# Hybrid attention and mLSTM block: attention one unit further ahead, mLSTM from unit 6, first output weights through four raw tiles

## The chip, the cores and the metric

One core of a Trainium2 chip runs the whole layer as one launch. The metric is the device time of one execution in microseconds (us), taken as the median of several runs. The engines are named as in the profile: PE is TensorE (matmuls), PEld its weight loads, DVE is VectorE, ACT is ScalarE, POOL is GpSimd, SP is the engine whose queue issues nearly all transfers.

## What is computed

The input is 2048 tokens of 1024 values. After an RMS norm one projection feeds two mixers; their outputs, each times a gate, are concatenated and projected back onto the residual, and a last RMS norm follows.

```python
h = rmsnorm(x, norm_g)
u = einsum("bsd,de->bse", h, w_in)
q_a, k_a, v_a, z_a, x_m, o_m, z_m = split(u, cuts)
# (A) 8 heads: causal windows of dilation 1, 4 and 16 with ALiBi, mixed by their softmax denominators
for window, dilation in ((128, 1), (512, 4), (2048, 16)):
    o, l = dilated_window_attention(q_a, k_a, v_a, window, dilation, slopes)
wts = softmax(stack(lses), axis=0)
att = sum(wts * stack(outs)) * silu(z_a)
# (B) 4 heads of an mLSTM matrix memory, chunk by chunk
hm = mlstm_chunkwise(q_m, k_m, v_m, log_i, log_f)
mls = groupnorm(sigmoid(o_m) * hm) * silu(z_m)
y = x + einsum("bse,ed->bsd", concatenate([att, mls]), w_out)
out = rmsnorm(y, final_g)
```

## The kernel before

**Stages.** First the input projection runs as a long stream of float32 products on PE, and its results go to DRAM. Then come three kinds of work that share the engines: attention, mLSTM, and the half of the output projection that belongs to the mLSTM. Last comes the other half of the output projection with the final norm.

**Attention** (`attention`) runs over 256 units, 32 for each of 8 heads; a unit is one block of 128 queries against a near window or a far one. For a unit `qk` makes the scores: three matmuls into the PSUM tile `pq` (two buffers), a DVE instruction that adds the bias and takes the row's extreme (L752), and an exponential on ACT (L754), which leaves the weights in the score tile `s` (three buffers). `flip` transposes them on PE (L762) into the PSUM tile `pt` (two buffers, which mLSTM uses too), and ACT or DVE copies them to `p` (L767, L765). `pv` multiplies them with the values (L780). In pass i of the loop stand `qk` of unit i, `flip` of unit i-2 and `pv` of unit i-3. After a head, `head_stats` and `head_merge` mix its two windows; `spread` broadcasts a row of weights over the partitions with a matmul whose stationary operand is the tile `sel` (L828).

**mLSTM** (`mlstm`) runs over 16 chunks of 128 tokens, two units a chunk, and `norm` closes each chunk with a chain of small DVE instructions. It is a generator of 400 steps.

**The early half of the output projection** (`early`) multiplies the mLSTM's output with the lower half of `w_out`, first for the left 512 columns (n=0), then for the right ones (n=1). It loads 8 weight tiles of 128x512 for each n into raw tiles `wor` (two buffers), and `split` makes of each a high part on ACT (L98) and a low part on DVE (L99) in `we`. The 16 blocks of mLSTM output come in halves the same way, through `wor` into `me` (three buffers). A block is 8 steps of three matmuls (L1142 to L1144) into `pu`; x is added and the sum goes to `y_d`. Between n=0 and n=1 the weights are changed.

**What sets the order.** The main loop at the end weaves the generators. `start` (18) attention units go alone; then, up to unit `end` (180), each attention unit is followed by its share of the 400 mLSTM steps; `lag` (3) units go alone; then 2.6 steps of `early` follow each attention unit, 2.0 after the last one. A step that yields 0 ends the share of its unit. From pass 230 on, `load_wo` also loads the upper half of `w_out`, through `wor` as well (and later a third raw tile, `qh`). This order is only a priority: a planner orders the instructions of each engine by it and by the times at which it expects operands and buffers to be ready, so an instruction that is ready may pass others that stand ahead of it in the text. On the chip each engine then runs its instructions strictly in the planned order. The pool `woB` of `early` takes over the memory of the mLSTM's pool `mp`, and `mp` that of the projection's pool (`ph`).

Of the kernel before, what the change touches and what calls it, by code (L numbers as in the profile page):

```python
# [8 lines left out]
F32 = mybir.dt.float32  # L9
# [18 lines left out]
def kernel(  # L28
# [693 lines left out]
    def qk(at, d, u):  # L722
        R, b = u
        g, r = b // 4, b % 4
        kh, kl, bl, st = d["kh"], d["k"], d["bl"], d["st"]
        ps = pq.tile([128, 512], F32, name="pq")
        if R:
            n = (g + 1) * 128
            bias = bl[:, 768 - n:768]
            col = 32 + b  # L730
            ks = lambda t: t[:, r * 512:r * 512 + n]
        else:
            n = 256 if b else 128
            bias = bl[:, 256 - n:256]
            col = b
            ks = lambda t: t.rearrange("p (r b j) -> p b r j", r=4, b=16)[:, max(b - 1, 0):b + 1]

        def keys(t):
            k = ks(t)
            if n == 128:  # L740
                k = k[:, None] if R else k
                k = k.to_broadcast([k.shape[0], 2, *k.shape[2:]])
            return k

        qhr, qlr = (d["qr", g][:, i, g % 2] for i in range(2))
        qh, ql = (t[:, r * 128:(r + 1) * 128] for t in ((qhr, qlr) if R else (qhi[:, g % 2], qt[:, g])))
        w = max(n, 256)
        nc.tensor.matmul(ps[:, 0:w], qh, keys(kh), start=True, stop=False)  # L748
        nc.tensor.matmul(ps[:, 0:w], qh, keys(kl), start=False, stop=False)  # L749
        nc.tensor.matmul(ps[:, 0:w], ql, keys(kh), start=False, stop=True)  # L750
        s = at.tile([128, 512], F32, name="s", bufs=3)
        nc.vector.tensor_tensor_reduce(s[:, :n], ps[:, :n], bias, 1.0, 3e38, ALU.add, ALU.min,  # L752
                                       accum_out=st[:, col:col + 1])
        nc.scalar.activation(s[:, :n], s[:, :n], AF.Exp, bias=st[:, col:col + 1], scale=-1.0,  # L754
                             accum_out=st[:, 16 + col:17 + col])
        return s, n
# [31 lines left out]
    def head_stats(at, d):  # L788
        h = d["h"]
        ps = pt.tile([128, 512], F32, name="pt")  # L790
        nc.tensor.transpose(ps[:64, :128], d["st"], ident)
        sr = at.tile([128, 512], F32, name="s", bufs=3)[:64, :128]
        nc.vector.tensor_copy(sr[:32].rearrange("p (r j) -> p r j", r=4), ps[:32, :128].rearrange("p (j r) -> p r j", r=4))
        nc.vector.tensor_copy(sr[32:], ps[32:64, :128])
        sd = st_d[h]
# [29 lines left out]

    def spread(d, n, q):
        pw = pt.tile([128, 512], F32, name="pt")
        nc.tensor.matmul(pw, sel[:, 2 * q + n // 2], d["wr"][:, n % 2 * 512:n % 2 * 512 + 512], start=True, stop=True)  # L828
        return residues(pw)

    def head_merge(at, d):
# [20 lines left out]
    def attention(at):  # L852
# [6 lines left out]
        D_ = {}  # L859
        S_ = {}  # L860
        P_ = {}
        for i in range(len(units) + 3):
            if i < len(units):
                h, u = units[i]
                if i == 0:
# [3 lines left out]
                    D_[0]["kh"] = kh  # L869
                    qk_split(D_[0], 0)  # L870
                S_[i] = qk(at, D_[h], u)
            if 0 <= i - 2 < len(units):
                h, u = units[i - 2]
                s, n = S_[i - 2]
                P_[i - 2] = flip(at, D_[h], u, s, n)
            if i >= 3:
                h, u = units[i - 3]
                pv(D_[h], u, P_.pop(i - 3), S_.pop(i - 3)[1])
            if i < len(units):
                h, (R, b) = units[i]  # L880
                if R and b % 4 == qlag and h + 1 < AH:
# [9 lines left out]
                if R and b % 4 == slag:  # L891
                    if b < 12:
                        qk_split(D_[h], b // 4 + 1)
                    elif h + 1 < AH:
                        qk_split(D_[h + 1], 0)
            if i % 32 == 3 and i > 31:
                stats = head_stats(at, D_[i // 32 - 1])
                next(stats)
            if i % 32 == 9 and i > 31:
                next(stats, None)  # L900
            if i % 32 == 4 and i > 31:
                merges.append(head_merge(at, D_[i // 32 - 1]))
            if merges and i % 32 >= 14 and next(merges[0], "end") == "end":
                merges.pop(0)
# [187 lines left out]
    def early():  # L1092
# [2 lines left out]
        M = {}  # L1095

        def w_get(n, e):
            raw["w", n, e] = woB.tile([128, 512], F32, name="wor", bufs=2)
            nc.sync.dma_start(raw["w", n, e], w_out[(KT + e) * 128:(KT + e + 1) * 128, n * 512:(n + 1) * 512])

        def w_split(n, e):
# [1 line left out]
            split(t[:, 0], t[:, 1], raw.pop(("w", n, e)))  # L1103

        def m_get(n, b, i):
            raw["m", n, b, i] = woB.tile([128, 512], F32, name="wor", bufs=2)
            nc.sync.dma_start(raw["m", n, b, i], mls_d[b, i])

        def m_split(n, b, i):
            t = M[n, b, i] = woB.tile([128, 2, 4, 128], F32R, name="me", bufs=3)  # L1110
            split(t[:, 0], t[:, 1], raw.pop(("m", n, b, i)).rearrange("p (e t) -> p e t", e=4))

        def x_get(n, b):
            raw["x", n, b] = woB.tile([128, 512], F32, name="xe", bufs=2)
# [1 line left out]

        seq = [(n, b) for n in range(2) for b in range(NB)]
        late = None
        w_get(0, 0)
        m_get(0, 0, 0)  # L1120
        w_split(0, 0)
        m_split(0, 0, 0)
        yield 0
        for e in range(1, 8):
            w_get(0, e)
            if e == 4:
                m_get(0, 0, 1)
                w_split(0, e)
                m_split(0, 0, 1)
            else:  # L1130
                w_split(0, e)
            if e % 2:
                yield 0
        for s, (n, b) in enumerate(seq):
            nxt = seq[s + 1] if s + 1 < len(seq) else None
# [3 lines left out]
            for e in range(8):  # L1139
# [9 lines left out]
                if swap:  # L1149
                    if e in (1, 2):  # L1150
                        w_get(1, e - 1)
                    if e >= 5:
                        w_split(1, e - 5)
                        w_get(1, e - 3)
                elif nxt:
                    if e in (0, 3):
                        m_get(*nxt, e // 3)
                    if e == 4:
                        m_split(*nxt, 0)
            xr = raw.pop(("x", n, b))  # L1160
            nc.vector.tensor_tensor(xr, xr, acc, ALU.add)
            late = (n, b, xr)
            if swap:
                for e in range(3, 8):
                    w_split(1, e)
                    if e < 6:
                        w_get(1, e + 2)
                    elif e < 8:
                        m_get(*nxt, e - 6)
                    yield 0  # L1170
                m_split(*nxt, 0)
                m_split(*nxt, 1)
                yield 0
            elif nxt:
                m_split(*nxt, 1)
        nc.sync.dma_start(y_d[late[1] * 128:(late[1] + 1) * 128, late[0] * 512:(late[0] + 1) * 512], late[2])

    def out_acc():
# [13 lines left out]
    def out_fin(pss, b):  # L1192
# [3 lines left out]
        for n in range(2):  # L1196
            cols = slice(n * 512, (n + 1) * 512)
            nc.vector.tensor_tensor(xr[:, cols], xr[:, cols], pss[n], ALU.add)
            jk = at.tile([128, 512], F32, name="s", bufs=3)
            nc.scalar.activation(jk, xr[:, cols], AF.Square, accum_out=s2[:, n:n + 1])  # L1200
        out_norm(xr, s2, b)

# [13 lines left out]
    def out_last(pss, b):  # L1216
# [3 lines left out]
        for n in range(2):  # L1220
# [1 line left out]
            for e in range(KT):  # L1222
                out_mm(pss, b, e, (n,))
            nc.vector.tensor_tensor(xr[:, cols], xr[:, cols], pss[n], ALU.add)
            jk = at.tile([128, 512], F32, name="s", bufs=3)
            nc.scalar.activation(jk, xr[:, cols], AF.Square, accum_out=s2[:, n:n + 1])
            if n == 0:
                nc.vector.tensor_tensor(xr[:, cols], xr[:, cols], fg[0], ALU.mult)
# [5 lines left out]
    accs = [0]  # L1234
    raws = [0, False]
    acc = {}
    total, done, start, end, lag = 16 * 25, 0, 18, 180, 3
    at = prex.enter_context(tc.tile_pool(name="at", bufs=1, side="right"))
    ax = []
    by_r = []  # L1240
    sel = at.tile([8, 4, 128], F32R, name="sel")
    nc.vector.tensor_tensor(sel, ident[:8, 0:4, None].to_broadcast([8, 4, 128]),
                            ident[:8, 4:8, None].to_broadcast([8, 4, 128]), ALU.add)
    work = attention(at)
    for i in range(start):
        next(work)
# [116 lines left out]
```

## Time and profile before

| | us |
|---|---|
| median of 3 runs | 2227.05 (2223.18 to 2228.98) |
| profiled execution | 2220.11 |
| its span, first to last instruction | 2217.2 |

| engine | busy us | share of the span |
|---|---|---|
| PE | 2126.7 | 96% |
| PEld | 1788.0 | 81% |
| DVE | 1488.1 | 67% |
| ACT | 942.8 | 43% |
| POOL | 251.8 | 11% |

All times within a run are us from the first instruction. The projection ends at about 1243; attention and mLSTM run side by side to about 1700, attention and the early half of the output projection from about 1727 to 1958, the rest of that half to 2034, and the other half to the end. The granted clock is the share of TensorE's full clock that was given in a stretch.

### The profile page before, as it was taken

The numbers are of one execution on the slowest core, as the hardware profiler recorded it, in microseconds if no ns is written. First come the engines' busy times: TensorE is split into PE (matmuls) and PEld (weight loads), VectorE is DVE, ScalarE is ACT, GpSimd is POOL, SyncE is SP. The second block draws the span as 40 slices with busy tenths as digits, with TensorE's granted clock in tenths as the row PEclk, the third lists the DMA queues.
The fourth block names the chain that finished last, engine by engine and source line by source line (L and its number), as shares of the span: only waits on it lengthen the run. The fifth ranks groups of instructions, "written<-read, shape, count | busy, mean of one in ns | idle before, by whom it ended". The sixth has DMA issues, their size and how long they took to land.

```text
span 2217.2 us, 32676 instructions
## 1 busy us (share of the span) xinstructions
PE 2126.7 (96%) x11826; PEld 1788.0 (81%) x11826; DVE 1488.1 (67%) x3050; ACT 942.8 (43%) x1905; POOL 251.8 (11%) x221
## 2 busy tenths in 40 slices
PE   5999999999999999999999999999898999999998
PEld 4777888998878888787779888888887788777886
DVE  8887768556696558576666578868777644643654
ACT  6433333333383223334344555655555645532221
POOL 2200000000000000000000223343342221210000
PEclk9999999999999999999999999999999999999999
DMA  4256343432263333343324677776675664565442
GB/s 154 95 177 190 114 159 115 158 114 101 90 204 133 114 114 105 125 138 115 133 77 160 186 203 208 213 234 188 195 211 178 192 184 157 173 193 176 162 138 86
DMA packets 278896, 341.52 MB, mean 154 GB/s; under 512 B 22224, under 2 KB 194704, under 8 KB 276688
## 3 DMA queue, kind: packets, MB, share of 16 engines
q1 hardware_dynamic: 277872, 338.85, 48.2%
q8 instruction: 93, 1.52, 0.3%
q10 hardware_dynamic: 864, 0.59, 0.1%
q14 instruction: 67, 0.55, 0.1%
HBM read 222.13 MB, written 117.24 MB: 153 GB/s over the span
## 4 chain that ended last, share of the span: by engine, by line
PE 74%; DVE 9%; DMA 8%; issue 5%; ACT 3%; POOL 1%; SPq 0%; ACTq 0%; DVEq 0%; POOLq 0%
PE pb L349 31%; PE pa L349 12%; PE pm L780 3%; PE pu L997 2%; PE pt L762 2%; PE pu L985 2%; DMA wor<-mls_d 2%; DMA wor<-in_w_out 1%; DMA k<-k_d 1%; PE aux L500 1%; PE aux L510 1%; PE pq L748 1%; PE pq L750 1%; PE pq L749 1%; PE pu L982 1%
## 5 line engine op out<-in xcount | busy, mean ns | idle before, releaser
L98 ACT ACTIVATE whi<-ws 128x1024 fp32r<-128x1024 f32 x140 | 148.2, 1059 | 376.5 <-PE pb L349 209.4
L99 DVE TENSOR_TENSOR wlo<-ws,whi 128x1024 fp32r<-128x1024 f32 x140 | 171.8, 1227 | 81.3 <-ACT whi L98 80.4
L139 DVE TENSOR_TENSOR ws<-w,w 128x1024 f32<-128x1024 f32 x140 | 172.1, 1229 | 24.0 <-DMA w<-in_w_in 22.4
L754 ACT ACTIVATE s<-s,st 128x256 f32<-128x256 f32 (+3 forms) x256 | 134.9, 527 | 76.0 <-DVE st L752 68.8
L411 DVE TENSOR_TENSOR o<-pb,o 128x1024 f32<-128x1024 f32 x84 | 102.8, 1224 | 92.9 <-PE pb L349 91.9
L752 DVE CUSTOM_DVE_ANT_0 s<-pq,bl 128x256 f32<-128x256 f32 (+3 forms) x256 | 114.2, 448 | 43.3 <-PE pq L750 32.0
L612 POOL COPY bl<-bl 128x256 f32<-128x256 f32 x8 | 6.4, 796 | 1150.5 <-DMA q<-q_d 1111.3
L767 ACT ACTIVATE p<-pt 128x256 f32<-128x256 f32 (+1 forms) x192 | 81.3, 424 | 105.7 <-PE pt L762 104.6
L762 PE MATMUL pt<-sc,s 128*128 128x128 f32 x568 | 107.7, 279 | 7.1 <-ACT p L767 5.3
L98 ACT ACTIVATE whi<-w 128x1024 fp32r<-128x1024 f32 x56 | 59.2, 1057 | 125.2 <-PE pb L349 118.7
L1142 PE MATMUL pu<-we,me 128*128 128x512 f32 x256 | 106.6, 417 | 5.3 <-ACT me L98 4.4
L411 DVE TENSOR_TENSOR o<-pa,o 128x1024 f32<-128x1024 f32 x56 | 68.4, 1221 | 62.8 <-PE pa L349 62.8
L1143 PE MATMUL pu<-we,me 128*128 128x512 f32 x256 | 102.1, 399 | 2.9 <-DVE me L99 2.9
L1144 PE MATMUL pu<-we,me 128*128 128x512 f32 x256 | 101.2, 395 | 0.0
L780 PE MATMUL pm<-p,vc 128*128 128x128 f32 x640 | 96.3, 281 | 3.3 <-DVE p L765 1.7
L404 ACT ACTIVATE o<-pb 128x1024 f32<-128x1024 f32 x84 | 84.9, 1016 | 15.6 <-DVE o L411 9.8
L780 PEld LDWEIGHTS pm<-p,vc 128*128 128x128 f32 x640 | 84.0, 195 | 7.0 <-ACT p L767 3.5
L99 DVE TENSOR_TENSOR wlo<-w,whi 128x1024 fp32r<-128x1024 f32 x56 | 68.3, 1220 | 27.5 <-ACT whi L98 27.5
L762 PEld LDWEIGHTS pt<-sc,s 128*128 128x128 f32 x568 | 72.7, 143 | 17.3 <-ACT p L767 6.7
L99 DVE TENSOR_TENSOR me<-wor,me 128x512 fp32r<-128x512 f32 x64 | 48.4, 758 | 56.0 <-ACT me L98 55.9
L780 PE MATMUL pm<-p,vn 128*128 128x128 f32 x496 | 78.7, 279 | 5.1 <-ACT p L767 5.1
L997 PE MATMUL pu<-v,kw 128*128 128x257 f32 x240 | 71.6, 401 | 9.4 <-DVE C L1000 4.8
(592 smaller groups left out, 6565.9 us busy)
## 6 DMA issues: line engine op xcount, KB each, us to landing
w<-in_w_in SPq DMA_DIRECT2D x112, 512.0 KB
wor<-mls_d SPq DMA_DIRECT2D x64, 256.0 KB
q_d<-o SPq DMA_DIRECT2D x8, 1024.0 KB
k_d<-o SPq DMA_DIRECT2D x16, 512.0 KB
vm_d<-vm SPq DMA_DIRECT2D x32, 256.0 KB
xc_d<-xc SPq DMA_DIRECT2D x32, 256.0 KB
qm_d<-qm SPq DMA_DIRECT2D x32, 256.0 KB
v_d<-o SPq DMA_DIRECT2D x8, 1024.0 KB
```

The costliest lines, as they stand in the source:

```text
L98: nc.scalar.activation(hi, raw, AF.Copy)
L99: nc.vector.tensor_tensor(lo, raw, f(hi), ALU.subtract)
L139: eng.tensor_tensor(s, a, b, ALU.add if sign > 0 else ALU.subtract)
L349: nc.tensor.matmul(out, lhsT, rhs, start=start, stop=stop, skip_group_check=True)
L411: nc.vector.tensor_tensor(dst, ps, src, op)
L752: nc.vector.tensor_tensor_reduce(s[:, :n], ps[:, :n], bias, 1.0, 3e38, ALU.add, ALU.min, accum_out=st[:, col:col + 1])
L754: nc.scalar.activation(s[:, :n], s[:, :n], AF.Exp, bias=st[:, col:col + 1], scale=-1.0, accum_out=st[:, 16 + col:17 + col])
L762: nc.tensor.transpose(pp[:, i * 128:(i + 1) * 128], s[:, i * 128:(i + 1) * 128], ident)
L780: nc.tensor.matmul(od, v, p[:, j * 128:(j + 1) * 128], start=j == 0, stop=j == m - 1)
L997: nc.tensor.matmul(u[:, 0:257], kw[:, 2 * i + e, :], v[:, i], start=True, stop=True)
L1142: nc.tensor.matmul(acc, m[:, 0, j], w[:, 0], start=e == 0, stop=False)
L1143: nc.tensor.matmul(acc, m[:, 1, j], w[:, 0], start=False, stop=False)
```

## The change

Attention gets a fourth score tile `s`, and `flip` and `pv` move one pass back: pass i holds `qk` of unit i, `flip` of unit i-3 and `pv` of unit i-4, so the loop has one pass more. `head_stats` and `head_merge` follow one pass later. To make room, `sel` shrinks from [8, 4, 128] to [8, 4], and `spread` reads a column of it with step 0 as the stationary operand. The mLSTM starts after 6 attention units instead of 18, and `lag` becomes 0. In `early` the first eight weight tiles use four raw tiles (`wor` and `xe` in turn) and are loaded four ahead of their split, with two yields instead of five before the first matmul. The mLSTM's output is loaded straight into the low part of `me` and split there in place, without a raw tile, one half after pass e=4 and the other after e=6; at the change from n=0 to n=1 three yields stand instead of six.

```diff
-        s = at.tile([128, 512], F32, name="s", bufs=3)
+        s = at.tile([128, 512], F32, name="s", bufs=4)
...
-        nc.tensor.matmul(pw, sel[:, 2 * q + n // 2], d["wr"][:, n % 2 * 512:n % 2 * 512 + 512], start=True, stop=True)
+        nc.tensor.matmul(pw, sel[:, 2 * q + n // 2:2 * q + n // 2 + 1].to_broadcast([8, 128]), d["wr"][:, n % 2 * 512:n % 2 * 512 + 512], start=True, stop=True)
...
-            if 0 <= i - 2 < len(units):
-                h, u = units[i - 2]
-                s, n = S_[i - 2]
-                P_[i - 2] = flip(at, D_[h], u, s, n)
-            if i >= 3:
+            if 0 <= i - 3 < len(units):
                 h, u = units[i - 3]
-                pv(D_[h], u, P_.pop(i - 3), S_.pop(i - 3)[1])
+                s, n = S_[i - 3]
+                P_[i - 3] = flip(at, D_[h], u, s, n)
+            if i >= 4:
+                h, u = units[i - 4]
+                pv(D_[h], u, P_.pop(i - 4), S_.pop(i - 4)[1])
...
         def w_get(n, e):
-            raw["w", n, e] = woB.tile([128, 512], F32, name="wor", bufs=2)
+            tag = ("wor", "xe")[e // 2 % 2] if n == 0 else "wor"
+            raw["w", n, e] = woB.tile([128, 512], F32, name=tag, bufs=2)
...
         def m_get(n, b, i):
-            raw["m", n, b, i] = woB.tile([128, 512], F32, name="wor", bufs=2)
-            nc.sync.dma_start(raw["m", n, b, i], mls_d[b, i])
+            t = M[n, b, i] = woB.tile([128, 2, 4, 128], F32R, name="me", bufs=3)
+            nc.sync.dma_start(f(t[:, 1]).rearrange("p e t -> p (e t)"), mls_d[b, i])
 
         def m_split(n, b, i):
-            t = M[n, b, i] = woB.tile([128, 2, 4, 128], F32R, name="me", bufs=3)
-            split(t[:, 0], t[:, 1], raw.pop(("m", n, b, i)).rearrange("p (e t) -> p e t", e=4))
+            t = M[n, b, i]
+            split(t[:, 0], t[:, 1], f(t[:, 1]))
...
-        w_get(0, 0)
-        m_get(0, 0, 0)
-        w_split(0, 0)
-        m_split(0, 0, 0)
-        yield 0
-        for e in range(1, 8):
-            w_get(0, e)
-            if e == 4:
-                m_get(0, 0, 1)
-                w_split(0, e)
-                m_split(0, 0, 1)
-            else:
-                w_split(0, e)
-            if e % 2:
+        for e in range(12):
+            if e >= 4:
+                w_split(0, e - 4)
+            if e < 8:
+                w_get(0, e)
+            if e % 4 == 3 and e < 8:
+                m_get(0, 0, e // 4)
+            if e in (4, 8):
+                m_split(0, 0, e // 4 - 1)
+            if e in (5, 9):
                 yield 0
...
-                elif nxt:
+                if nxt:
                     if e in (0, 3):
                         m_get(*nxt, e // 3)
-                    if e == 4:
-                        m_split(*nxt, 0)
+                    if e in (4, 6):
+                        m_split(*nxt, e // 2 - 2)
...
-                    elif e < 8:
-                        m_get(*nxt, e - 6)
-                    yield 0
-                m_split(*nxt, 0)
-                m_split(*nxt, 1)
-                yield 0
-            elif nxt:
-                m_split(*nxt, 1)
+                    if e % 2:
+                        yield 0
...
-    total, done, start, end, lag = 16 * 25, 0, 18, 180, 3
+    total, done, start, end, lag = 16 * 25, 0, 6, 180, 0
...
-    sel = at.tile([8, 4, 128], F32R, name="sel")
+    sel = at.tile([8, 4], F32R, name="sel")
```

## Rows read from the trace of the kernel before

**Rows 1.** Windows by stage: length, PE, PEld, DVE, ACT, POOL busy, clock, DMA share, GB/s
```profile
200.00:1243.00 1043.00, 1039.66 (x5892) 875.52 (x5890) 699.25 (x775) 397.50 (x496) 1.80 (x3) 1.00 0.38 126
1243.00:1268.00 25.00, 23.02 (x153) 21.20 (x153) 14.73 (x55) 18.03 (x59) 11.35 (x11) 0.86 1.03 294
1268.00:1699.00 431.00, 402.10 (x2631) 358.62 (x2631) 333.22 (x1264) 251.44 (x759) 143.04 (x136) 0.98 0.71 208
1699.00:1746.00 47.00, 41.08 (x236) 33.26 (x235) 33.06 (x89) 26.20 (x73) 18.22 (x14) 0.89 0.54 168
1746.00:1958.00 212.00, 205.37 (x1144) 171.19 (x1143) 113.60 (x279) 106.94 (x270) 40.08 (x29) 1.00 0.57 177
1958.00:2034.00 76.00, 70.29 (x283) 52.90 (x281) 35.19 (x61) 17.83 (x29) 12.41 (x8) 0.98 0.63 200
2034.00:2208.00 174.00, 173.94 (x753) 141.40 (x753) 91.68 (x256) 36.49 (x91) 0.00 (x0) 1.00 0.40 130
```

**Rows 2.** Waits of PE, 1268 to 1699: waiter, releaser, total us, times, longest
```profile
PE pu L997 <- DVE C L1000: 4.8, 3, 2.9
PE pm L780 <- ACT p L767: 4.6, 3, 2.9
...
PE pt L762 <- ACT p L767: 3.6, 2, 2.2
PE pt L970 <- ACT p L767: 2.7, 1, 2.7
```

**Rows 3.** Tile s: who waited for it, us and times
```profile
  PEld pt L762: 0.5, 2
```

**Rows 4.** Waits of ACT, 1268 to 1699
```profile
ACT s L754 <- DVE st L752: 39.5, 35, 4.3
```

**Rows 5.** Windows of line L752 alone: DVE busy (two instructions a unit), clock, DMA
```profile
1243.00:1268.00 25.00, 8.22 (x40) 0.86 1.03 294
1268.00:1699.00 431.00, 70.18 (x310) 0.98 0.71 208
...
1746.00:1958.00 212.00, 28.70 (x126) 1.00 0.57 177
```

**Rows 6.** Windows, ten us around the end of the mLSTM
```profile
1710.00:1720.00 10.00, 8.21 (x37) 7.10 (x36) 6.27 (x24) 2.75 (x8) 2.82 (x2) 0.53 0.38 123
```

**Rows 7.** Waits of PE, 1699 to 1746
```profile
PE pt L1036 <- DVE hm L1031: 1.2, 1, 1.2
...
PE pu L1142 <- ACT we L98: 0.8, 1, 0.8
```

**Rows 8.** Timeline of SP, 1715 to 1730: start, us, line, transfer
```profile
1720.56 0.37 SPq L1099 DMA_DIRECT2D wor<-in_w_out  x1
...
1727.95 1.79 SPq L1099 DMA_DIRECT2D wor<-in_w_out  x2
```

**Rows 9.** Tile me, its splits on ACT: ns least, median, most
```profile
L98 ACT ACTIVATE me<-wor x64: 615/631/634, 1726.2 to 2028.5; 128x512 fp32r<-128x512 f32 x64
```

**Rows 10.** Waits of ACT, 1746 to 2034
```profile
ACT me L98 <- DMA wor<-mls_d: 57.0, 24, 6.6
...
ACT me L98 <- PE pu L1144: 16.4, 13, 2.5
```

**Rows 11.** Waits of PE, 1746 to 2034
```profile
PE pu L1142 <- ACT me L98: 4.4, 3, 1.6
...
PE pu L1143 <- DVE me L99: 1.7, 5, 0.8
```

**Rows 12.** Chain of waits, 1746 to 2036: start, us, what
```profile
1764.99 2.60 DMA wor<-mls_d
...
1800.70 5.60 DMA wor<-mls_d
...
2003.76 4.67 DMA wor<-mls_d
```

**Rows 13.** Line L828, weight loads of sel: ns least, median, most
```profile
L828 PEld LDWEIGHTS pt<-wr,sel x64: 181/181/280, 1342.7 to 1998.1; 8*128 8x128 f32 x64
```

More of the change, by code (lines that the diff above doesn't have):

```diff
@@ L791, in head_stats @@
         nc.tensor.transpose(ps[:64, :128], d["st"], ident)
-        sr = at.tile([128, 512], F32, name="s", bufs=3)[:64, :128]
+        sr = at.tile([128, 512], F32, name="s", bufs=4)[:64, :128]
         nc.vector.tensor_copy(sr[:32].rearrange("p (r j) -> p r j", r=4), ps[:32, :128].rearrange("p (j r) -> p r j", r=4))
@@ L861, in attention @@
         P_ = {}
-        for i in range(len(units) + 3):
+        for i in range(len(units) + 4):
             if i < len(units):
@@ L895, in attention @@
                         qk_split(D_[h + 1], 0)
-            if i % 32 == 3 and i > 31:
+            if i % 32 == 4 and i > 31:
                 stats = head_stats(at, D_[i // 32 - 1])
@@ L900, in attention @@
                 next(stats, None)
-            if i % 32 == 4 and i > 31:
+            if i % 32 == 5 and i > 31:
                 merges.append(head_merge(at, D_[i // 32 - 1]))
@@ L1198, in out_fin @@
             nc.vector.tensor_tensor(xr[:, cols], xr[:, cols], pss[n], ALU.add)
-            jk = at.tile([128, 512], F32, name="s", bufs=3)
+            jk = at.tile([128, 512], F32, name="s", bufs=4)
             nc.scalar.activation(jk, xr[:, cols], AF.Square, accum_out=s2[:, n:n + 1])
@@ L1224, in out_last @@
             nc.vector.tensor_tensor(xr[:, cols], xr[:, cols], pss[n], ALU.add)
-            jk = at.tile([128, 512], F32, name="s", bufs=3)
+            jk = at.tile([128, 512], F32, name="s", bufs=4)
             nc.scalar.activation(jk, xr[:, cols], AF.Square, accum_out=s2[:, n:n + 1])
@@ L1240 @@
     by_r = []
-    sel = at.tile([8, 4, 128], F32R, name="sel")
-    nc.vector.tensor_tensor(sel, ident[:8, 0:4, None].to_broadcast([8, 4, 128]),
-                            ident[:8, 4:8, None].to_broadcast([8, 4, 128]), ALU.add)
+    sel = at.tile([8, 4], F32R, name="sel")
+    nc.vector.tensor_tensor(sel, ident[:8, 0:4], ident[:8, 4:8], ALU.add)
     work = attention(at)
```

## The prediction

> **What bounds the kernel now.** I read the windows by stage first, then the waits of PE, then those of ACT, the engine that PE waits for most; the chain of waits last, for the places where a transfer stands in it.
>
> In the windows the reader is to see that PE is the engine of this kernel: busy for the whole projection and the whole last stage, with 3.3 us and 0.06 us idle in them [rows 1]. The change touches neither. What can be won lies between 1243 and 2034, and I count it in two parts: idle time of PE, and the clock. A mean granted clock of 0.98 says that PE stood part of the time at the lower of its two levels, 1.2 GHz, where work takes twice as long as at 2.4, so the time lost is the length times (1 - clock).
>
> By stage, idle plus clock [rows 1]: 1243 to 1268, attention alone, 2.0 + 25 x 0.14 = 5.5 us; 1268 to 1699, attention beside mLSTM, 28.9 + 431 x 0.02 = 37.5; 1699 to 1746, the handover to the early half of the output projection, 5.9 + 47 x 0.11 = 11.1; 1746 to 1958, attention beside that half, 6.6; 1958 to 2034, its rest, 5.7 + 1.5 = 7.2. Together 68 us, 3.1% of the span: no reordering can win more, and since the amount of matmul work doesn't change, it can win by these losses alone.
>
> In the mLSTM stage the idle time of PE ends with DVE freeing an mLSTM buffer (4.8 us on one line), or with ACT copying `p` [rows 2]: 4.6 + 3.6 + 2.7 = 10.9 us. ACT is late with `p` not because it is full (251 of 431 us) but because it runs in order and stands 39.5 us, in 35 places, before an exponential whose scores DVE has not yet delivered [rows 4].
>
> **The change part by part.** I cost it against the profiled execution, 2220.11 us with a span of 2217.2; that is 6.9 us below the median of 2227.05, so what I find is taken off the median.
>
> **One unit further ahead, a fourth score tile.** It removes no instruction and adds one pass, in which only the last `pv` stands. It lengthens the way from the exponential to the transpose. But transposes hardly wait for `s`: 0.5 us in two places, on the weight load's side [rows 3]. The copies of `p`, for which PE does wait, still come one pass before their `pv`. So the direct gain is nothing; an indirect one is that the planner may put other work between the exponentials that hold ACT. The most that this is worth is all 10.9 us of those waits and their part of that stage's clock loss, 8.6 x 10.9/28.9 = 3.2, so 14 us. At the other end a new plan may put one more bubble where the clock falls: 1710 to 1720 ran at 0.53 and lost 4.7 us by it [rows 6]. I take 2 us of gain, near the row of 0.5; ends 14 gain, 5 loss. The Trainium skill (Perfetto Trace Analysis, section Optimization Strategy) holds that gaps which repeat on the engine that should be saturated can mean that buffers are too few for the next tile. By that the fourth tile would return most of the 10.9 us, while the trace puts these gaps on another tile.
>
> **mLSTM from unit 6.** The 400 steps spread over 174 units instead of 162, 2.30 a unit instead of 2.47. Attention alone took 25 us for 20 units, 1.25 us each, the mixed stage 431 us for 155 units, 2.78 each [rows 5]. So 12 x 1.25 = 15 us of attention move into the mixed stage. Does that thin DVE out? It is busy 333 of 431 us, 77.3%; attention alone needs 14.73/20 = 0.74 us a unit [rows 1, 5], so afterwards (333 + 8.8)/(431 + 15) = 76.6%. Less than a point, on a loss of 37.5 us: 1 us of gain. The first loads of the mLSTM move into the one stretch where the DMA engines are full (1.03, 294 GB/s), past the loads of heads 0 and 1 on SP's queue; what hides that is attention work that is ready. Ends: the 2.0 us of idle time there gained, 4 us lost if a start-up bubble of the size of that stretch's 3.5 us of clock comes twice.
>
> **Handover.** Three units without `early` and three of five empty yields go, so the first matmul of `early` moves by count from unit 188 to 182. But the raw tiles lie in the mLSTM's memory: the first weight load goes out at 1720.56, and the next not before 1727.95, when one of two raw tiles is free [rows 8]. Four raw tiles let four loads go at once, and those 7.4 us are where PE is short of work. On the other side ten splits of 0.63 us on ACT [rows 9], 6.3 us, fall into two units instead of five, ahead of the exponentials. Of the 11.1 us I take 3 as gained: the 0.8 us wait for the weights [rows 7] and half of the clock loss of 4.7 [rows 6]; the 1.2 us for the end of the mLSTM's norm stays. Ends 8 gain, 6 loss (all of the splits uncovered).
>
> **mLSTM output straight into `me`.** The same 64 splits, the same 64 loads, no raw tile. The load of a block's second half now waits on SP until PE has done four steps of the block before, since only then its buffer is free, and behind it on SP's queue stand x, y_d and the loads of q and k. Before, the load went ahead into a raw tile and ACT waited for the buffer, 16.4 us in 13 places [rows 10]. That wait goes; what is late next is the landing, for which ACT waits 57.0 us in 24 places already. PE feels this little: 4.4 + 1.7 us [rows 11]. I take nothing; ends 3 gain and the price of the third rival.
>
> **The rest of the early half.** By counting the yields, `early` has 21 of 256 steps left when attention's passes are done; afterwards none, since it starts 6 units earlier and has 3 empty yields fewer in its middle. In the chain of waits this stretch is a row of transfers through the two raw tiles, of 4.67 us for instance, each followed by its split [rows 12], and the upper half of `w_out` queues for the same tiles. Afterwards the raw tiles are free for `w_out`, so products of the last stage can be ready to fill gaps. Of 7.2 us I take 4; ends 7 gain, 5 loss (with nothing of `early` left as cover, one landing of 5.6 us stands bare).
>
> **`sel` as a column with step 0.** 64 weight loads of 181 ns [rows 13]. Nothing for the load of as many rows; were each doubled, 11.6 us, most of it beside the matmul before. Ends 0 and 5 loss.
>
> Sum: 2 + 1 + 3 + 0 + 4 = 10 us gained. The profiled execution would be 2210, the median 2227 - 10 = **2217 us**, with 2208 to 2222 as this case's own range.
>
> **The rivals.** *Nothing that can be measured.* The losses sit on mLSTM's DVE chains and in a plan that is drawn up anew; bubbles move and their sum stays. For it: the two largest terms rest on places of 7 and 11 us. Time 2227, 2221 to 2233.
>
> *A larger gain.* ACT's stops no longer reach PE: 14 us from the first part instead of 2, and 8 from the handover instead of 3, so 27 in all, 2200. Against it: transposes do not wait for `s`.
>
> *Slower, by the loads into `me`.* Mechanism: ACT stands before a split whose load could only start when PE freed the buffer. It decides from this point: between load and split lie three steps. At 2.6 steps a unit and 212/63 = 3.37 us a unit [rows 5] that is 3.9 us, less 0.3 for the issue, 3.6 us; landings in the chain take 2.6 to 5.6 us [rows 12], so they straddle it, and in the tail, where a step is three matmuls of 174/753 = 0.23 us [rows 1], three steps are 2.1 us and every landing is late. Price: 2.4 us (57.0/24) at each of 64 splits is 154 us of ACT instead of 73. If PE's waits for `me`, 6.1 us, and those for `p` grow in the same ratio, about 10 us, and one clock drop of 4.7 comes with it, that is 15; the tail's 4 us is not gained and 6 are: 2227 + 9 = 2236 us. The Trainium skill (DMA: Bandwidth & Descriptors, rules for kernel authors) advises issuing a transfer early and waiting late so that its fixed cost is hidden, about 2 us by its anatomy section (told there for transfers that GpSimd issues); that speaks against this edit, and by it 64 x 2 = 128 us of ACT would be open, an estimate from that page, near the 154 from the rows.
>
> *The change doesn't do what it says*: the fourth tile is never needed, because a plan never runs that far ahead. Then the first term is nothing and the time 2219, inside the forecast's range.
>
> **How the numbers follow.** Forecast 2217 (the unused tile included) 0.45; larger gain 0.08; nothing measurable 0.24; slower 0.23. A measurement here tells about 0.3%, 6.7 us, from no change. A small part of the forecast's range lies within that, against a small part of the second case beyond it: faster 0.52, same 0.25, slower 0.23. The range reaches to the larger gain's 2202 and a little past the slower case's time, 2238.
>
> **What would show it.** First part: ACT's 39.5 us before exponentials and PE's 10.9 us for `p` fall; if only the weight load's 0.5 us goes, the tile did nothing. mLSTM: its first matmul comes before 1269 or the early start was in vain. Handover: four weight loads issued together, and no stretch of ten us at 0.53. `me`: ACT's wait for `mls_d` against 57.0 us in 24 places; more than double and the third rival is at work. Tail: the loads of `w_out` before 2000 and no transfers in the chain there. The prediction is wrong if the mixed stage's loss of 37.5 us moves by more than 10 either way, since I gave it 3.

## The result, and the profile after

The changed kernel takes 2242.88 us in the median (2236.72 to 2247.88) where the kernel before takes 2224.54; the ratio is 1.0079, with a 95% interval of 1.0064 to 1.0094. By the ratio it is 17.6 us slower (0.0079 x 2224.5), where 10 us of gain were forecast. The profiled execution took 2247.88 us, 5 above its median; that of before lay 4 below its own, so the two profiles differ by more than the medians do.

The windows by stage of the changed kernel, cut where its own stages end (attention before mLSTM; the mixed stage; the handover; attention beside the early half; the rest of that half), columns as in [rows 1]:

```profile
1244.00:1270.00 26.00, 9.71 (x53) 8.71 (x54) 9.89 (x29) 10.12 (x30) 8.92 (x10) 0.68 1.02 276
1270.00:1749.00 479.00, 433.84 (x2793) 384.35 (x2792) 365.79 (x1340) 270.89 (x811) 152.90 (x142) 0.96 0.66 193
1749.00:1780.00 31.00, 28.80 (x154) 22.33 (x153) 19.82 (x40) 18.35 (x44) 10.96 (x8) 1.00 0.62 204
1780.00:2006.00 226.00, 219.12 (x1235) 183.44 (x1234) 115.42 (x287) 111.99 (x281) 42.35 (x31) 1.00 0.56 176
2006.00:2065.00 59.00, 55.35 (x217) 40.42 (x216) 33.90 (x57) 17.39 (x29) 12.13 (x8) 0.97 0.68 215
```

Look at the first row first. In the stretch where the kernel before had PE busy 23 of 25 us [rows 1], it is now busy 9.7 of 26: 16.3 us are idle. The clock is at 0.68, but its 26 x 0.32 = 8.3 us may not simply be added, as the prediction adds them: a low clock costs only where PE has work. Here is the part of the stretch in which PE stands still, in the changed kernel, and then the whole stretch of the kernel before, from the projection's last product to 2 us behind the mLSTM's first matmul:

```profile
1254.00:1268.20 14.20, 0.02 (x1) 0.03 (x1) 2.94 (x4) 2.88 (x6) 3.46 (x6) 0.59 0.96 337
```

```profile
1241.70:1271.00 29.30, 24.64 (x165) 22.44 (x164) 18.22 (x60) 22.29 (x67) 12.51 (x12) 0.88 0.95 273
```

Of the 8.3 us of clock, 14.2 x 0.41 = 5.8 fall into the standstill and cost nothing. So the start loses 16.3 + 2.5 = 19 us, against 4.7 + 29.3 x 0.12 = 8 in the kernel before. The second row loses 45.2 + 479 x 0.04 = 64 us. The same cut of the kernel before, from 2 us behind the mLSTM's first matmul to its last:

```profile
1271.00:1717.00 446.00, 415.11 (x2692) 368.97 (x2693) 345.14 (x1312) 256.14 (x778) 148.35 (x141) 0.97 0.70 206
```

That is 30.9 + 13.4 = 44 us. The remaining stages lose 2, 7 and 5 us where those of the kernel before, cut alike, lose 4, 7 and 7. So two places are worse: the start, by some 11 us, and the mixed stage, by 20.

**The start.** The timeline of PE around the mLSTM's first matmul (L962); the bracket is the idle time before it and what ended it:

```profile
1253.63 0.39 PE L780 MATMUL pm<-p,vc 128*128 128x128 f32 x2
1268.20 2.05 PE L962 MATMUL pt<-q,xc 128*128 128x128 f32 x8 [14.18 <-DMA xc<-xc_d]
1270.04 0.63 PE L762 MATMUL pt<-sc,s 128*128 128x128 f32 x2
```

ACT in the same stretch, and SP's queue:

```profile
1253.06 0.19 ACT L754 ACTIVATION_READ_ACCUMULATOR s<-s,st 128x1 f32 x1
1263.02 2.19 ACT L625 ACTIVATE kh<-k 128x512 fp32r<-128x512 f32 x4 [9.77 <-DMA k<-k_d]
```

```profile
1251.23 0.38 SPq L455 DMA_DIRECT2D o_d<-o  x1
...
1254.25 0.51 SPq L611 DMA_DIRECT2D bl<-in_alibi_c  x1
1260.46 0.80 SPq L929 DMA_DIRECT2D nb<-nb_d  x2
1261.31 0.43 SPq L932 DMA_DIRECT2D q<-qm_d  x1
1261.78 0.43 SPq L934 DMA_DIRECT2D xc<-xc_d  x1
```

PE stands 14.18 us before an mLSTM matmul whose operand has not landed; this wait is called the stop below. ACT stands 9.77 us before a key tile that has not landed either. Behind the waiting matmul in PE's planned order stand transposes of scores (L762) whose exponentials ACT had finished by 1253.3. The mLSTM's first matmul starts at 1268.2; in the kernel before it started at 1269.0, after a wait of only 0.9 us. The early start has gained that matmul less than a microsecond. What it has moved is the order: PE's planned order has the score products of 10 units ahead of that matmul, where the kernel before has those of 22.

**The mixed stage.** PE's waits there, columns as in [rows 2], then ACT's, as in [rows 4], both from 1270 to 1727:

```profile
PE pu L997 <- DVE sm L990: 12.9, 10, 3.2
PE pu L997 <- DVE C L1000: 8.3, 6, 2.8
...
PE pm L780 <- ACT p L767: 2.5, 1, 2.5
```

```profile
ACT s L754 <- DVE st L752: 67.3, 67, 3.3
```

PE's waits for `p` fell, but those for DVE at the mLSTM's state products rose from some 9 us to 21, and ACT stands 67.3 us before exponentials; in the kernel before it was 39.5 us [rows 4], or 42.3 over its mixed stage as cut here.

### The profile page after: what moved, and what is told of

Its sections match the earlier page's. It is cut to its first block, busy times and chain, and to the rows that moved or that the text cites. A ratio compares the mean times of both kernels' runs of the same rounds, so it can differ in the third digit from the quotient of the medians.

```text
span 2246.1 us, 32570 instructions
## 1 busy us (share of the span) xinstructions
PE 2129.9 (95%) x11826; PEld 1788.4 (80%) x11826; DVE 1497.7 (67%) x3050; ACT 947.6 (42%) x1905; POOL 253.9 (11%) x221
## 5 line engine op out<-in xcount | busy, mean ns | idle before, releaser
L752 DVE CUSTOM_DVE_ANT_0 s<-pq,bl 128x256 f32<-128x256 f32 (+3 forms) x256 | 114.3, 447 | 34.9 <-PE pq L750 29.9
L762 PE MATMUL pt<-sc,s 128*128 128x128 f32 x568 | 107.3, 279 | 9.6 <-DVE E L963 5.0
L99 DVE TENSOR_TENSOR me<-me 128x512 fp32r<-128x512 f32 x64 | 52.3, 819 | 73.8 <-ACT me L98 71.2
L762 PEld LDWEIGHTS pt<-sc,s 128*128 128x128 f32 x568 | 72.7, 143 | 19.2 <-DVE E L963 5.6
```

The lines of the kernel that those rows point to most:

```text
L99: nc.vector.tensor_tensor(lo, raw, f(hi), ALU.subtract)
L762: nc.tensor.transpose(pp[:, i * 128:(i + 1) * 128], s[:, i * 128:(i + 1) * 128], ident)
```

## Experiments

Three theories. **A**, the stop at the start: the whole loss is the order of PE there. **B**, the extra unit of attention makes the mixed stage worse. **C**, the loads into `me` hold ACT, the third rival of the prediction. Four runs take the change apart.

**start 18.** The changed kernel with one number put back.

```diff
-    total, done, start, end, lag = 16 * 25, 0, 6, 180, 0
+    total, done, start, end, lag = 16 * 25, 0, 18, 180, 0
```

> The changed kernel with one number put back: the mLSTM starts after 18 attention units instead of 6. Theory A (the stop at the start): the changed kernel loses its time at 1254 to 1268, where PE stands 14.2 us before the mLSTM's first matmul for a transfer that lands at the same time as in the kernel before, with only 10 score products planned ahead of it instead of 22. Then this run is within 0.3% of the kernel before, some 17 us faster than the changed kernel, and the stop is under 3 us. Theory B (the mixed stage): one unit further ahead makes PE wait longer for DVE at the mLSTM's state products, 22 us on line L997 instead of 9; then this run stays 0.4% or more slower than before, and those waits stay. Theory C (the loads into me): likewise still 0.4% or more slower, but with the loss after 1727.

Measured 2224.35 us, ratio 1.0001 (0.9986 to 1.0016). The stop is 1.09 us:

```profile
1266.28 1.13 PE L962 MATMUL pt<-q,xc 128*128 128x128 f32 x8 [1.09 <-DMA xc<-xc_d]
```

The loss goes with the start, as A says; B and C fall as its causes. That all of it sat in the stop is not shown: the mixed stage of this run loses 35.9 + 13.6 = 50 us, where that of the changed kernel lost 64.

**Start 6 alone**, in the kernel before.

```diff
-    total, done, start, end, lag = 16 * 25, 0, 18, 180, 3
+    total, done, start, end, lag = 16 * 25, 0, 6, 180, 3
```

> The kernel before with one number changed: the mLSTM starts after 6 attention units, nothing else. Theory A: 0.5% to 1.0% slower than before (11 to 22 us), with a stop of PE of 10 to 15 us before the mLSTM's first matmul. Theories B and C: within 0.3% of before, since neither the score tiles nor the early half of the output projection differ.

Measured 2240.58 us, ratio 1.0069 (1.0051 to 1.0087), 15.4 us slower. The stop, and the windows of its start and its mixed stage:

```profile
1266.77 2.04 PE L962 MATMUL pt<-q,xc 128*128 128x128 f32 x8 [12.13 <-DMA xc<-xc_d]
```

```profile
1241.70:1268.80 27.10, 12.07 (x60) 10.78 (x60) 10.99 (x29) 11.35 (x31) 9.92 (x10) 0.68 1.03 275
1268.80:1736.80 468.00, 426.58 (x2797) 376.80 (x2796) 361.90 (x1341) 267.59 (x813) 151.41 (x143) 0.99 0.69 197
```

The start has 15.0 us idle, 10 more than the kernel before; the mixed stage loses 41.4 + 4.7 = 46, near the 44 of before. One number of the change, put alone, brings the stop and costs 15.4 us, where the whole change costs 17.6.

**Attention's part alone**: the edits to `s`, `flip`, `pv`, `head_stats`, `head_merge` and `sel`, in the kernel before.

```diff
-        s = at.tile([128, 512], F32, name="s", bufs=3)
+        s = at.tile([128, 512], F32, name="s", bufs=4)
...
-            if 0 <= i - 2 < len(units):
+            if 0 <= i - 3 < len(units):
...
-            if i >= 3:
+            if i >= 4:
```

> The kernel before with only attention's part of the change: four score tiles, transposes and value products one pass later, the small sel. Theory A: 0 to 9 us faster than before, or no difference. Theory B: 0.4% or more slower (9 us), with PE's waits for DVE on line L997 near 22 us instead of 9. My forecast for this part was 2 us of gain, ends 14 gain and 5 loss.

Measured 2226.86 us, ratio 1.0003 (0.9990 to 1.0016). Of PE's waits in its mixed stage the longest is one that a fourth tile should have shortened, if any:

```profile
PE pt L762 <- ACT p L767: 10.4, 3, 5.2
PE pu L997 <- DVE sm L990: 5.6, 5, 2.3
```

B falls: the waits for DVE are those of the kernel before. ACT's wait before exponentials rises in this run, from 42.3 us to

```profile
ACT s L754 <- DVE st L752: 58.9, 57, 3.4
```

and still the part does nothing to the time that can be measured. (The profiled execution of this run, 2234.93 us, was its slowest.)

**The early half's part alone**: the edits to `early`, and lag 0, in the kernel before.

```diff
-    total, done, start, end, lag = 16 * 25, 0, 18, 180, 3
+    total, done, start, end, lag = 16 * 25, 0, 18, 180, 0
```

> The kernel before with only the early half's part of the change: four raw tiles for the first weights, the mLSTM's output straight into me, fewer empty yields, lag 0; mLSTM still from unit 18, attention as before. Theory A: 0 to 9 us faster than before (my forecast for these parts was 3 + 0 + 4 = 7 us). Theory C: 0.4% or more slower, ACT's waits for the mLSTM's output well above the 57 us of before.

Measured 2217.02 us, ratio 0.9973 (0.9959 to 0.9987): 6 us gained. ACT's and PE's waits from 1746 to 2045, its first weight loads on SP, and its tail from the last value product to the last step of `early`:

```profile
ACT me L98 <- DMA me<-mls_d: 60.9, 31, 5.7
```

```profile
PE pu L1139 <- ACT me L98: 3.3, 4, 2.1
PE pu L1140 <- DVE me L99: 2.1, 6, 0.7
```

```profile
1726.53 0.85 SPq L1100 DMA_DIRECT2D wor<-in_w_out  x2
1727.42 1.11 SPq L1100 DMA_DIRECT2D xe<-in_w_out  x2
```

```profile
1978.70:2036.70 58.00, 55.15 (x220) 39.59 (x219) 32.60 (x56) 16.59 (x28) 13.03 (x8) 1.00 0.71 225
```

C falls too: ACT waits for the landings about as long as before (57.0 us [rows 10]). The four first loads go out together, and the tail loses 2.9 us instead of 7.2. Where the 6 us are gained no row can say: the profiled execution took 2221.77 us, more than the 2220.11 of the kernel before.

Four more runs ask what makes the stop. Its loads wait on SP from 1254.8 to 1260.5 for the projection's memory, and the DMA engines are full.

**The last store first**: `run_post(1000)` ahead of the first attention unit, so that the store `o_d` stands in front of eight of the nine transfers of head 0.

```diff
+    run_post(1000)
     for i in range(start):
         next(work)
-        run_post(1)
-    run_post(1000)
```

> The changed kernel with the projection's last store (o_d, 1 MB) issued behind the first transfer of head 0 instead of behind all nine. In the changed kernel SP's queue stands from 1254.8 to 1260.5 before the mLSTM's first loads, whose memory is that store's source. Theory A1 (memory): the stop of PE before the mLSTM's first matmul comes from that wait; it shrinks from 14.2 by 4 to 6 us, and the time by as much. Theory A2 (bytes): the DMA engines are full (1.02, 276 GB/s) until the loads land, whichever transfer stands in front; the stop shrinks by 2 us at most.

Measured 2246.35 us, ratio 1.0093 (1.0070 to 1.0116). SP, and PE:

```profile
1257.31 1.51 SPq L929 DMA_DIRECT2D nb<-nb_d  x2
1259.40 0.32 SPq L932 DMA_DIRECT2D q<-qm_d  x1
1260.24 0.32 SPq L934 DMA_DIRECT2D xc<-xc_d  x1
```

```profile
1256.12 0.68 PE L780 MATMUL pm<-p,vn 128*128 128x128 f32 x4 [3.00 <-DMA vn<-v_d]
1257.19 0.39 PE L780 MATMUL pm<-p,vn 128*128 128x128 f32 x2
1270.15 1.20 PE L962 MATMUL pt<-q,xc 128*128 128x128 f32 x4 [12.28 <-DMA q<-qm_d]
```

The loads were issued up to 3 us sooner and landed 2 us later, and attention's values came late as well. So A2 fits and A1 does not: it is the bytes, and in this full stretch what one transfer gained another lost.

**One transfer fewer**: `zs` of head 0, 1 MB, at unit 20.

```diff
-        nc.sync.dma_start(d["zs"], za_d[h])
+        if h:
+            nc.sync.dma_start(d["zs"], za_d[h])
...
+            if i == 20:
+                nc.sync.dma_start(D_[0]["zs"], za_d[0])
```

> The changed kernel with one transfer of 1 MB (zs of head 0, needed only after the head's end) taken out of the full stretch and issued at unit 20. A1 and A2 both: 1 MB at 276 GB/s is 3.6 us, so the stop shrinks from 14.2 to 10 to 11 us. If the stop were not set by the transfers at all, it would stay.

Measured 2240.36 us, ratio 1.0079 (1.0061 to 1.0098), no change that can be told from the changed kernel's. The stop fell by 2.9 us, a little short of what was expected, to

```profile
1265.51 2.08 PE L965 MATMUL pt<-q,xc 128*128 128x128 f32 x8 [11.24 <-DMA xc<-xc_d]
```

where 1 MB at the mean rate would be 3.6. Transfers set the length of the stop; taking 1 MB of them away is not the remedy.

**Loads at 6, steps at 18**: the mLSTM's loads and first step stay at unit 6, the other steps follow from unit 18.

```diff
-            while done < total * (i + 1 - start) // (end - start) and next(side, "end") != "end":
+            while done < max(1, total * (i + 1 - 18) // (end - 18)) and next(side, "end") != "end":
```

> The changed kernel with the mLSTM's loads and its first step left at unit 6, but its further steps only from unit 18, so that 22 score products instead of 10 stand ahead of the mLSTM's first matmul in PE's plan. Theory A (order on PE): the stop is under 3 us and the time within 0.3% of the kernel before (2225), though the loads are issued no earlier than in the changed kernel. If the loads' place on the queue were the harm, the time would stay near 2243.

Measured 2227.01 us, ratio 1.0013 (0.9997 to 1.0028). The stop is gone:

```profile
1267.21 1.13 PE L962 MATMUL pt<-q,xc 128*128 128x128 f32 x8 [0.69 <-DMA xc<-xc_d]
```

The loads have the same place as in the changed kernel; only PE has the score products of 22 units ahead of the matmul again. So the harm is PE's order, and the early loads alone win nothing.

**start 12**, with everything else changed.

```diff
-    total, done, start, end, lag = 16 * 25, 0, 6, 180, 0
+    total, done, start, end, lag = 16 * 25, 0, 12, 180, 0
```

> The changed kernel with the mLSTM from unit 12, half way; 16 score products stand ahead of its first matmul. Theory A: each attention unit put ahead covers about 1.25 us, so the stop is 14.2 - 6 x 1.25 = 6 to 8 us and the time 7 to 9 us below the changed kernel, about 2234.

Measured 2213.27 us, ratio 0.9958 (0.9944 to 0.9972). The stop is near what was expected, the time 21 us better:

```profile
1267.74 2.04 PE L962 MATMUL pt<-q,xc 128*128 128x128 f32 x8 [8.34 <-DMA xc<-xc_d]
```

```profile
1269.70:1713.50 443.80, 418.18 (x2752) 369.43 (x2750) 343.94 (x1325) 264.03 (x795) 148.54 (x141) 0.99 0.72 207
```

Its mixed stage loses 25.6 + 4.4 = 30 us, not 44 or 64. Theory A explains the stop but not this. Two further theories: **S**, a wider spread of the mLSTM's steps leaves DVE more room; **P**, each variant is planned anew and its mixed stage scatters.

The next four have only another start: 12 in the kernel before, 13 and 9 in the changed one, 19 in the kernel before.

> The kernel before with the mLSTM from unit 12 and nothing else. The changed kernel with start 12 has a stop of 8.3 us and is still the fastest, since its mixed stage loses 30 us instead of 44 before and 64 in the changed kernel. Theory S (spread): steps spread over 168 units instead of 162 leave DVE more room; then this run gains too, its stop of 6 to 8 us paid back: 0.995 to 1.000 of before, with a mixed-stage loss under 38 us. Theory P (plan): every variant gets a new planned order whose loss in the mixed stage scatters by some 10 us whatever the start; then this run is before plus the stop, 1.000 to 1.005.

Measured 2220.24 us, ratio 0.9989 (0.9975 to 1.0004). The stop is 6.0 us and the mixed stage loses 35: S's signs, though the interval reaches into P's.

> The changed kernel with the mLSTM from unit 13, the neighbour of the fastest variant. Theory S: a smooth curve, 2211 to 2217 us, stop about 7 us, mixed-stage loss near 30 us. Theory P: the stop is about 7 us too, but the mixed-stage loss is anywhere between 30 and 50 us and the time between 2212 and 2232.

Measured 2214.72 us, ratio 0.9959 (0.9944 to 0.9974). The stop is 7.6 us. The time fits both; the mixed stage's 40 us fit P.

> The changed kernel with the mLSTM from unit 9; 13 score products stand ahead of its first matmul. Theory A on the stop: between 14.2 us at start 6 and 8.3 at start 12, so 10 to 12 us. Theory S: the mixed-stage loss stays near 30 us or below, since the spread is wider still, and the time is 2215 to 2222. Theory P: the time is anywhere between 2215 and 2240.

Measured 2233.36 us, ratio 1.0037 (1.0018 to 1.0055). The stop is 10.4 us, as A has it; the time, and 51 us in the mixed stage, go against S.

> The kernel before with the mLSTM from unit 19, a change of one unit that takes away no work and adds no stop. Theory S: within 0.2% of before. Theory P: the new order alone moves the mixed-stage loss by 5 us or more either way, and the time with it by 0.2% or more.

Measured 2232.36 us, ratio 1.0040 (1.0025 to 1.0056). No work was added and no stop, and yet 9 us are lost, with the same waits grown as in the changed kernel (from 1271 to 1725):

```profile
PE pu L997 <- DVE C L1000: 12.8, 5, 4.9
PE pu L997 <- DVE sm L990: 9.5, 10, 2.2
```

S as a smooth curve falls by this run and by start 9. P is right that a new order alone moves the time.

Then the question whether the mixed stage's loss belongs to the order or to the execution: both kernels once more, unaltered.

> The changed kernel once more, unaltered, for a second profile of the same planned order. Its first profile lost 25.5 us (idle and clock of PE) at the start and 64 in the mixed stage, against 8 and 44 before. Theory P (the loss belongs to the planned order): 55 to 65 us in the mixed stage again. Theory E (it belongs to the single execution): 40 to 50 us, and only the start's 25 us come back.

> The kernel before once more, unaltered, for a second profile. Theory P: 40 to 48 us lost in the mixed stage, as in the first. Theory E: anywhere between 35 and 60.

The changed kernel again 2243.72 us, ratio 1.0102 (1.0076 to 1.0128); the kernel before again 2222.45, 0.9996 (0.9977 to 1.0014). Their mixed stages, the changed kernel first, and the longest wait of PE in the changed one's:

```profile
1270.00:1746.00 476.00, 429.29 (x2801) 380.70 (x2800) 365.85 (x1341) 270.15 (x811) 153.37 (x143) 0.97 0.67 194
```

```profile
1271.00:1717.00 446.00, 416.30 (x2690) 370.11 (x2691) 346.48 (x1311) 257.20 (x779) 148.25 (x140) 0.97 0.69 206
```

```profile
PE pu L997 <- DVE sm L990: 16.5, 11, 4.2
```

46.7 + 14.3 = 61 us and 29.7 + 13.4 = 43, beside 64 and 44 the first time: the loss belongs to the planned order and comes back with its waits. (In both profiles of a kernel PE's 11826 matmuls, and the instructions of DVE and ACT, stand in the same order.)

Last, which part carries the gain at start 12: the early half's part without attention's, and attention's without the early half's.

> The kernel before with the early half's part of the change and the mLSTM from unit 12; attention as before. If the parts add up, this is the early part's 0.9973 times start 12's 0.9989: 0.996, as good as the changed kernel with start 12 (0.9958), and one unit further ahead does nothing. If the extra unit carries the gain, it is 0.998 or above.

Measured 2210.36 us, ratio 0.9936 (0.9912 to 0.9960), **the lowest of all, 14 us below the kernel before**. That is better than either expectation, but its interval ends where the parts' product lies (0.996) and overlaps that of the changed kernel with start 12 (0.9958), so all it says of attention's part is that no gain by it shows here. Its start has a stop of 5.48 us; its mixed stage loses 24.9 + 8.9 = 34 us:

```profile
1270.00:1716.00 446.00, 421.14 (x2749) 374.12 (x2748) 346.92 (x1326) 261.78 (x795) 148.22 (x141) 0.98 0.71 207
```

> The kernel before with attention's part of the change and the mLSTM from unit 12; the early half as before. If the parts add up: 1.0003 times 0.9989, 0.999. If one unit further ahead pays only where a stop has to be made good, 0.997 or below.

Measured 2216.23 us, ratio 0.9970 (0.9955 to 0.9985). That is the second expectation; but against start 12 alone (0.9989) the intervals overlap, so a gain by attention's part is not shown here either.

The variants by their start, with the units whose score products stand ahead of the mLSTM's first matmul in PE's planned order, the stop before it, and the mixed stage's loss (idle plus clock of PE, from 2 us behind that matmul to the mLSTM's last):

| start | kernel | units ahead | stop us | mixed stage us | ratio |
|---|---|---|---|---|---|
| 6 | changed | 10 | 14.2 | 64 | 1.0079 |
| 6 | before, start alone | 10 | 12.1 | 46 | 1.0069 |
| 9 | changed | 13 | 10.4 | 51 | 1.0037 |
| 12 | changed | 16 | 8.3 | 30 | 0.9958 |
| 12 | before, early part | 16 | 5.5 | 34 | 0.9936 |
| 12 | before, attention part | 16 | 8.2 | 34 | 0.9970 |
| 12 | before, start alone | 16 | 6.0 | 35 | 0.9989 |
| 13 | changed | 17 | 7.6 | 40 | 0.9959 |
| 18 | changed | 22 | 1.1 | 50 | 1.0001 |
| 18 | before | 22 | 0.9 | 44 | 1 |
| 18 | before, early part | 22 | 0.7 | 46 | 0.9973 |
| 18 | before, attention part | 22 | 1.9 | 50 | 1.0003 |
| 19 | before, start alone | 23 | none | 50 | 1.0040 |

The stop falls by 1 us for each unit of the start, (14.2 - 8.3)/6. Each mixed-stage value is from one execution, up to 8 us off its kernel's median, and the rounding of the clock alone leaves 2 us, so differences of some 5 us say nothing. Even so the five runs with start 12 or 13 have the five lowest values, 30 to 40, against 43 to 64 in all others; why there, no run settles.

## Why the prediction was wrong

The forecast was 2217 us with a range of 2202 to 2238; 2242.88 were measured.

**mLSTM from unit 6: the step that failed.** I gave it 1 us of gain and at worst 4 of loss; alone it costs 15.4 us. I wrote that what hides the mLSTM's first loads "is attention work that is ready". Ready it was, but it stood behind the waiting matmul in PE's order, and a fixed order makes such work no cover. The numbers lay in my own rows: with the DMA engines full at 294 GB/s [rows 1] it was to be expected that the first matmul, at 1269, would hardly come sooner for being asked sooner (it came at 1266.8 with start 6 alone and at 1266.3 with start 18 in the changed kernel), and 12 units at 1.25 us [rows 5] are 15 us of attention that I moved from before the matmul to behind it. I counted these 15 us as work that changes place, when they were the cover of a wait that does not change place. The sign to look for was named, its first matmul before 1269 "or the early start was in vain". It came at 1268.2: met by the letter, and the start was in vain all the same, for the sign did not ask what PE did until then. The clock added little to the price: most of its low time fell into the stop, and the mLSTM's first eight matmuls took 2.05 us instead of 1.13. For the same reason the prediction's sum of idle time and length times (1 - clock) counts some time twice wherever PE stands still at a low clock.

**The mixed stage** was the other miss. I gave 3 us to a loss of 37.5 and said that 10 either way would make the prediction wrong. Cut alike, it rose from 44 to 64 us, and from 43 to 61 in the second pair of profiles. That DVE's share hardly changes was right (0.774 before, 0.764 after, 0.766 forecast), but the loss does not follow DVE's share; it belongs to the planned order, as the repeated profiles and start 19 show. With start 18 the same change loses 50 us there. Why this order is the worst of them stays open.

**One unit further ahead**: 2 us of gain forecast, none measured (0.9990 to 1.0016), within the ends. The row on which I leaned, 0.5 us of waiting for `s` [rows 3], was the right one to read for the direct gain. The indirect gain was not there: ACT's wait before exponentials and PE's waits for `p` were to fall; with this part alone the first rose to 58.9 us and the second, at the transposes, from 3.6 to 10.4. The Trainium skill's rule (Perfetto Trace Analysis, section Optimization Strategy), that repeated gaps can mean too few buffers, would have given most of 10.9 us; the runs side with the row. ACT's longer wait by itself does not decide the mixed stage: it is 51.2 us in the changed kernel with start 12, whose mixed stage loses least. The small `sel` cost nothing: its weight loads take 180 ns in the changed kernel, 181 before [rows 13].

**The early half**: 3 + 0 + 4 = 7 us of gain forecast for its three parts, 6.0 measured (3.1 to 9.1). That the sum came out is in part luck, for two of the mechanisms did not. In the tail no step of `early` was to be left behind attention's last value product; 66 of the 256 stood there, and in the kernel before 89, where I had counted 21. The first two lines below show them (a step has one matmul on that line of the program), first for the kernel before, 1956 to 2036, then for the early half's part alone, 1978.7 to 2037.2; the third line is a landing that still stands in the chain of waits of that run's tail:

```profile
L1142 PE MATMUL pu<-we,me 128*128 128x512 f32 x89 | 36.6, 411 | 2.9 <-ACT me L98 2.9
```

```profile
L1139 PE MATMUL pu<-we,me 128*128 128x512 f32 x66 | 27.1, 410 | 1.0 <-ACT me L98 1.0
```

```profile
2027.73 5.04 DMA me<-mls_d
```

The tail's loss of 2.9 us instead of 7.2 is no sure gain either: other runs with the same part lose 2.2 (the changed kernel again), 5.4 (the changed kernel) and 8.2 (start 18). In the handover the four loads went out together as said, but of the 11.1 us that I laid to it only 3.7 lie behind the mLSTM's end. With the early half's part alone they are 3.6, and `early`'s first matmul starts 14.0 us behind that end instead of 10.5. The third rival, whose 2236 us came near the measured time by luck, was not at work: ACT's wait for the mLSTM's output is 56.4 us in the changed kernel, where more than double was its sign.

```profile
ACT me L98 <- DMA me<-mls_d: 56.4, 34, 5.0
```

So the sign of the forecast fell by one term: alone, the parts give -6 and 0 us, and the start about +15. But the parts do not simply add. Start 18 has 1.0001 with both other parts, where 0.9973 x 1.0003 = 0.9976 was to be expected, so without the early start, too, the forecast's gain would not have come; and with it 17.6 us were lost, where -6, 0 and +15 make 9.

## What to carry to other kernels

Work that is ready covers a wait only if it stands ahead of the waiting instruction in its engine's own order; so before a step is started earlier, ask when its operand lands, and if full DMA engines set that, count the work that the earlier place puts behind it, unit by unit, as lost cover. Read the stage that a step is moved into as well as the one it leaves: here the place was better at 12 than at 18 or 6. And where a planner draws up the order anew, a change of one unit can cost 0.4% by itself, so a gain of that size should be tried at neighbouring settings before it is put down to its idea.

## What the runs showed of the hardware

From the projection's end to the mLSTM's first matmuls the DMA engines had a busy share of 0.94 to 1.05 in all profiles, and the core moved 263 to 295 GB/s. The one other order of the same transfers that was tried did not bring the mLSTM's operand sooner. A share of 1 is not one rate: in the changed kernel 207 GB/s were moved from 1244 to 1253 and 388 from 1253 to 1263; what sets the rate, no run settles.

```profile
1244.00:1253.00 9.00, 6.89 (x38) 6.05 (x39) 6.56 (x24) 6.99 (x23) 5.46 (x4) 0.81 1.08 207
1253.00:1263.00 10.00, 1.02 (x10) 0.83 (x8) 0.39 (x2) 0.25 (x2) 2.17 (x4) 0.68 1.05 388
```

After the stops of 5.5 to 14.2 us the mLSTM's first eight matmuls took 2.04 to 2.08 us, where 1.13 were enough after those of 0.7 to 1.9 us: 1.8 times as long. In the changed kernel the granted clock was 0.50 while they ran (1268.2 to 1270), which is the lower of the clock's two levels, 1.2 GHz instead of 2.4.
